# Moving four of ten block-pair loads from GpSimd's casting queue to ScalarE's queue and ScalarE's cast

## The chip, the cores and the metric

The kernel runs on one core of one Trainium2 chip. The metric is the device time of one execution in microseconds (us); of several runs the median is taken. The profile is of one execution on the same core, and its times count from the start of its span.

## The reference

A batch of 16 sequences of 512 rows and 768 columns is multiplied by one 768 x 768 weight, and each of the 12 heads (64 columns) is then rotated with a cosine and a sine that depend on the row alone. All inputs and the output are fp32.

```python
y = np.matmul(x, weight)                       # (16, 512, 768) x (768, 768)
y = y.reshape(batch, seq, n_heads, head_dim)
y1, y2 = y[..., :32], y[..., 32:]
out1 = y1 * cos1 - y2 * sin1
out2 = y2 * cos2 + y1 * sin2
out = np.concatenate([out1, out2], axis=-1).reshape(batch, seq, hidden)
```

## The kernel before

**Tiles and groups.** The 8192 rows are 64 tiles of 128 rows, numbered `i`. Four tiles make a group `g` (0 to 15; `LAST` is 15). A tile takes its 128 rows with a stride of 4, so all tiles of a group use the same rows of cosine and sine. A pair is half a group, written `(g, h)` with `h` 0 or 1.

**The way of an ordinary tile.** SP loads it in fp32 into one of ten `xs` buffers (`load`, L210). ScalarE casts it to fp16 (`cast`: CAST `xc<-xs`, L190). PE transposes it in 12 pieces into PSUM (`turn_rows`: `pt`, L271), ScalarE copies the result to SBUF (COPY `xt<-pt`, L190), and PE multiplies it with the weight (`one`, L362), two halves of the contraction on the two halves of the array's rows, in two lines that `both` interleaves.

**The way of a block pair.** The pairs in `BLOCKS`, (5,1) to (13,1) and (15,1), are not transposed by PE. A quarter of the pair at a time is loaded by a DMA whose order of rows and columns does the coarse part of the transpose (`load_quarter`, L225), each quarter on 32 partitions. DVE then transposes blocks of 32 x 32 (`turn_pair`: STREAM_TRANSPOSE `xp<-...`, L299), 32-bit words that each hold two fp16 numbers. Before that the pair must be fp16, and this is done in two ways:

- `"sp"` pairs (5, 7, 9, 11, 13 and 15) are loaded in fp32 by SP into one of three `xb` buffers, and ScalarE casts and reorders them into `xd` (`cast_pair`: CAST `xd<-xb`, L190).
- `"pool"` pairs (6, 8, 10 and 12) are loaded by GpSimd, and the DMA casts on its way into one of three fp16 buffers `xh`. DVE's transpose reads `xh` directly.

**After the product.** DVE multiplies PSUM with cosine and sine in one instruction (`rope`, L419, into `tq` or `w_raw`), GpSimd adds the two halves into one of four output buffers `ov` (L445, the groups listed as POOL). The additions of the last groups are cut smaller. Stores (`store`, L477) of half a group are issued from ScalarE's queue up to group 12, then from SP's. An output buffer is written again four groups later, once its store has landed.

**What sets the order.** The order of each engine's instructions is written out by a loop over the tiles; the helper `do` adds the waits that the named buffers call for. The end of a tile `i` of the main loop is:

```python
        bturns(i + (B_AHEAD if i < QB * (LAST - 2) else 9))
        ...
        turns(i + 1 + (T_AHEAD if i > QB else 2), 1)
        casts(i + 1 + (C_AHEAD if i > QB else 4), 1 + i % 2)
        pool_loads(i + P_AHEAD)
        for q in stores.get(i, ()):
            store(*q)
```

So at tile `i` ScalarE's stream holds the COPY of tile `i + 3`, the casts up to tile `i + 5` (a block pair's cast at its first tile) and then a store, if one is due there. `casts` also calls `pump`, which hands SP's loads out in a fixed order. GpSimd's quarters are issued 20 tiles ahead of the pair (`P_AHEAD`). A queue's instructions wait in order: what stands behind a waiting one waits too.

Of the kernel before, what the change touches and what calls it, by code (L numbers as in the profile page):

```python
# [10 lines left out]
FP32 = mybir.dt.float32  # L11
FP16 = mybir.dt.float16
# [4 lines left out]
class Flow:  # L17
# [24 lines left out]
    def do(self, e, make, reads=(), writes=(), dma=None, tick=True, after=0):  # L42
        need = {}
        for k in reads:
            for s, v in self.wrote.get(k, {}).items():
                need[s] = max(need.get(s, 0), v)
        for k in writes:
            for d in (self.wrote, self.readby):
                for s, v in d.get(k, {}).items():
                    need[s] = max(need.get(s, 0), v)  # L50
        if e == "pe":
            need.pop("pe", None)
            if after:
                need["pe"] = after
        waits = self.settle(e, need)
        for s, v in waits[:-1]:
            self.eng[e].wait_ge(self.sem(s), v)  # L57
        i = make(self.eng[e])
        if waits:
            s, v = waits[-1]  # L60
            i.wait_op(self.sem(s), v, "sem-ge")
        name, step = (dma, 16) if dma else (e, 1)
        self.sem(name)
        self.order[name] = len(self.order) + sum(self.count.values())
        at = self.count[name] + step
        if tick or dma:
            i.then_inc(self.sems[name], step)
            self.count[name] = at
            self.known[name, at] = dict(self.seen[e])
        for k in reads:  # L70
            d = self.readby.setdefault(k, {})
            d[name] = max(d.get(name, 0), at)
        for k in writes:
            self.wrote[k] = {name: at}
            self.readby[k] = {}
        return i
# [32 lines left out]
def kernel(  # L109
# [11 lines left out]
    f = Flow(nc, tc)  # L121
    do = f.do
    P = nc.NUM_PARTITIONS

    B, S, H = x.shape
# [4 lines left out]
    NQ = P // R  # L130
    NT = H // (2 * P)
    SB = S // P
    QB = 4
# [5 lines left out]

    BLOCKS = {}  # L140
    for g in range(5, 14):
        BLOCKS[g, 1] = "pool" if g % 2 == 0 and g >= 4 else "sp"
    BLOCKS[LAST, 1] = "sp"

    def sbuf(name, shape, dt):
        return nc.alloc_sbuf_tensor(name, shape, dt).ap()

    NX, NB, NBH, NC, NCP, NXT, NXP, NOV = 10, 3, 3, 5, 2, 8, 4, 4

    ident = sbuf("ident", [P, P], FP16)  # L150
    cold = sbuf("cold", [P, 512], FP16)
# [2 lines left out]
    w_raw = sbuf("w_raw", [P, NT, 2, H], FP32)  # L154
    w_sb = sbuf("w_sb", [P, NT, 2, H], FP16)
    xs_b = [sbuf(f"xs{i}", [P, H], FP32) for i in range(NX)]
    xb_b = [sbuf(f"xb{i}", [P, 2 * H], FP32) for i in range(NB)]
    xh_b = [sbuf(f"xh{i}", [P, 2 * H], FP16) for i in range(NBH)]
    xc_b = [sbuf(f"xc{i}", [P, H], FP16) for i in range(NC)]
    xd_b = [sbuf(f"xd{i}", [P, 2 * H], FP16) for i in range(NCP)]  # L160
    xt_b = [sbuf(f"xt{i}", [P, NT, 2, P], FP16) for i in range(NXT)]
# [21 lines left out]
    def ring(name, n, state={}):  # L183
        k = state.get((id(f), name), 0)
        state[id(f), name] = k + 1
        return k % n
# [6 lines left out]
    def where(i):  # L193
        g, s = divmod(i, QB)
        return QB * (g // SB) + s, g % SB

    def pair_of(i):
        return i // QB, (i % QB) // 2

    def is_block(i):  # L200
        return pair_of(i) in BLOCKS

    xs, xc, xT = {}, {}, {}
# [10 lines left out]
    def load_quarter(gh, q):  # L214
        g, h = gh
        b, r = where(g * QB + 2 * h)
        e = BLOCKS[gh]
        src = x[b : b + 2].rearrange("b (j a r) (q k) -> r q a (b j) k", r=SB, a=R, q=NQ)
        if q == 0:
            xs[gh] = ring("xh", NBH) if e == "pool" else ring("xb", NB)  # L220
        k = xs[gh]
        name = f"xh{k}" if e == "pool" else f"xb{k}"
        buf = xh_b[k] if e == "pool" else xb_b[k]
        dst = buf.rearrange("p (j k) -> p j k", j=2 * NQ)
        do(e, lambda eng: eng.dma_start(out=dst[ts(q, R)], in_=src[r, q]),  # L225
           writes=[f"{name}q{q}"], dma=name)
# [52 lines left out]
    def cast_pair(gh, e="act"):  # L279
        k = xs[gh]  # L280
        c = ring("xd", NCP)
        xc[gh] = c
        do(e, copy(e, xd_b[c].rearrange("p (t j e) -> p t j e", t=NT, e=2),
                   xb_b[k].rearrange("p (j t e) -> p t j e", t=NT, e=2)),
           reads=[f"xb{k}q{q}" for q in range(NQ)], writes=[f"xd{c}"])

    def turn_pair(gh):
        g, h = gh
        z = ring("xp", NXP)
        dst = xp_b[z].bitcast(FP32)  # L290
        if BLOCKS[gh] == "pool":
            k = xs[gh]
            src = xh_b[k].bitcast(FP32).rearrange("p (j t) -> p t j", t=NT)
            rd = [f"xh{k}q{q}" for q in range(NQ)]
        else:
            c = xc[gh]
            src, rd = xd_b[c].bitcast(FP32), [f"xd{c}"]
        v = xp_b[z].rearrange("p (t m e) -> p t e m", t=NT, e=2)
        do("dve", lambda eng: eng.transpose(out=dst, in_=src), reads=rd, writes=[f"xp{z}"])  # L299
        for s in (0, 1):  # L300
            xT[g * QB + 2 * h + s] = (
                lambda t, e, s=s: v[:, t, e, ts(s, P)], f"xp{z}")
# [211 lines left out]
    xs_used, xb_used = [0], [0]  # L514
# [38 lines left out]
    def castx(i, e):  # L553
        cast(i, e)
        xs_used[0] += 1
# [33 lines left out]
    pump()  # L589

    rows_on = [False]
    state = {"cast": 4, "turn": 4, "bturn": 0, "pool": 0}
    pairs = sorted(BLOCKS)
    pool_pairs = [p for p in pairs if BLOCKS[p] == "pool"]

    def casts(upto, most=NTILE):
        while state["cast"] < min(upto, NTILE) and most > 0:
            most -= 1
            i = state["cast"]
            state["cast"] += 1  # L600
            if not is_block(i):
                castx(i, "act")
            elif i % 2 == 0 and BLOCKS[pair_of(i)] == "sp" and pair_of(i) not in xc:
                cast_pair(pair_of(i))
                xb_used[0] += 1
            pump()

    def turns(upto, most=NTILE):
# [12 lines left out]
            turn_pair(gh)  # L621
            state["bturn"] += 1

    def pool_loads(upto):
        while state["pool"] < len(pool_pairs):
            gh = pool_pairs[state["pool"]]
            if gh[0] * QB + 2 * gh[1] >= upto:
                return
            for q in (0, 2, 1, 3):
                load_quarter(gh, q)  # L630
            state["pool"] += 1

    stores = {}
    for g in range(LAST):
        for h in (0, 2):
            i = QB * (g + 1) + h
            q = (g, h * H, (h + 2) * H, "act")
# [4 lines left out]
            elif g < LAST - 2:  # L642
                i = QB * (LAST - 2) + 2 * (g - LAST + 4) + h // 2
            else:
                q = q[:3] + ("sp",)
            stores.setdefault(i, []).append(q)

    C_AHEAD, T_AHEAD, B_AHEAD, P_AHEAD = 5, 3, 4, 20
    ROWS = QB * LAST - 2

    for i in (0, 1):
# [3 lines left out]
    mm0(2, CHUNKS[5])  # L655
    rope(0, U0[2])
    casts(6)
    for c in CHUNKS[:3]:
        mm0(3, c)
# [8 lines left out]
    for i in range(QB, NTILE):  # L668
        g, s = divmod(i, QB)
        us = units(g)  # L670
        done_to = (s + 1) * H
        rows_on[0] = QB <= i <= QB * LAST
        if i == QB * (LAST - 2) + 2:
            cast_pair((LAST, 1))
            xb_used[0] += 1
        if i < ROWS:
            if s % 2 == 0:
                for r in range(2):
                    lines[r].extend(walk(i // 2, r))
            for n in range(1, 4):  # L680
                both((i - QB) * 4608 + n * 1536)
                if n == (1 if i > QB else 2):
                    turns(i + T_AHEAD, 1)
        if i == ROWS:
            both(NTILE * 4608)
        for n, p in enumerate(pieces(g, s)) if i >= ROWS else ():
            a, z, _, bank = p
            if n == 1 and i < QB * LAST:
                turns(i + T_AHEAD, 1)
            for c in CHUNKS:  # L690
                mm_piece(i, p, c, c == CHUNKS[0], c == CHUNKS[-1],
                         tick=c == CHUNKS[-1])
            for u in us:
                if u[1] == z:
                    rope(g, u)
        bturns(i + (B_AHEAD if i < QB * (LAST - 2) else 9))
        if i == 2 * QB:
            do("pool", lambda eng: eng.tensor_copy(out=ident32, in_=ident),
               reads=["ident"], writes=["ident32", "wr20"])
        turns(i + 1 + (T_AHEAD if i > QB else 2), 1)  # L700
        casts(i + 1 + (C_AHEAD if i > QB else 4), 1 + i % 2)
        pool_loads(i + P_AHEAD)
        for q in stores.get(i, ()):
            store(*q)
        if g == LAST:
            if s == 2:
                store(g, 0, H, "sp")
            if s == 3:
                store(g, H, 2 * H, "act")
# [44 lines left out]
```

## Time and profile before

| | |
|---|---|
| Time, three runs | 149.74, 150.99, 157.2 us; median 150.99 |
| Span of the profiled execution | 148.2 us (its own time is not listed apart; the runs lie 1.5 us and more above the span) |
| Busy: PE, DVE, POOL, ACT | 140.8, 126.0, 121.8, 79.0 us |
| Granted clock of TensorE, mean | 0.998 |
| Moved by DMA | 51.67 MB, mean 349 GB/s |
| Queues, share of 16 DMA engines' span | SP 57.0%, ACT 35.9%, POOL 8.6% |
| Issue to landing, median: tiles, SP's quarters, POOL's quarters, ACT's stores | 16.4, 16.4, 12.1, 9.6 us |

L followed by a number is a line of the kernel. PE is TensorE's matmul, PEld its weight load, DVE VectorE, ACT ScalarE, POOL GpSimd, SP SyncE; a q behind a name (ACTq) is the engine's sequencer, where DMAs are issued. A line of the profile's groups gives line, engine, operation, output and input by name with the buffer number left out, shape and count; then the busy time and the mean of one in ns; then the engine's idle time just before, with what ended it. In a timeline a row is a start, a duration, the engine, the operation, a count where several follow each other, and in brackets the idle time before it. A DMA share over 1 means that packets overlap.

### The profile page before, as it was taken

The numbers are of one execution on the slowest core, as the hardware profiler recorded it, in microseconds if no ns is written. First come the engines' busy times: TensorE is split into PE (matmuls) and PEld (weight loads), VectorE is DVE, ScalarE is ACT, GpSimd is POOL, SyncE is SP. The second block draws the span as 40 slices with busy tenths as digits, with TensorE's granted clock in tenths as the row PEclk, the third lists the DMA queues.
The fourth block names the chain that finished last, engine by engine and source line by source line (L and its number), as shares of the span: only waits on it lengthen the run. The fifth ranks groups of instructions, "written<-read, shape, count | busy, mean of one in ns | idle before, by whom it ended". The sixth has DMA issues, their size and how long they took to land.

```text
span 148.2 us, 4422 instructions
## 1 busy us (share of the span) xinstructions
PE 140.8 (95%) x1948; PEld 112.7 (76%) x1948; DVE 126.0 (85%) x99; ACT 79.0 (53%) x94; POOL 121.8 (82%) x73
## 2 busy tenths in 40 slices
PE   6789999999999999999999999999999999999980
PEld 2335578888888888888888888888888888765860
DVE  0335998886988899899989998999989999999991
ACT  3453898777777933557261915375263919931010
POOL 1000396999999998999999999879699999999990
PEclk9999999999999999999999999999999999999999
DMA  3999999999999999999999999999999999998675
GB/s 124 352 395 403 402 406 398 373 379 296 317 366 330 352 353 277 294 408 287 319 355 397 379 323 358 365 408 324 381 365 337 411 409 416 410 408 333 264 297 180
DMA packets 27555, 51.67 MB, mean 349 GB/s; under 512 B 6160, under 2 KB 13072, under 8 KB 27536
## 3 DMA queue, kind: packets, MB, share of 16 engines
q1 hardware_dynamic: 15824, 28.84, 57.0%
q10 hardware_dynamic: 7360, 20.97, 35.9%
q0 software_dynamic: 4352, 1.57, 8.6%
q8 instruction: 15, 0.25, 0.7%
q14 instruction: 4, 0.03, 0.1%
HBM read 27.79 MB, written 25.17 MB: 357 GB/s over the span
## 4 chain that ended last, share of the span: by engine, by line
PE 78%; DVE 12%; DMA 4%; issue 1%; SPq 1%; DVEq 0%
PE py L362 68%; DVE tq L419 8%; PE py L337 5%; PE pt L271 4%; DMA w_raw<-in_weight_dram 4%; DVE w_raw L419 2%; SPq L210 1%; PE pt L256 1%; DVE ov L445 1%; DVE xs L419 1%; SPq L232 1%; DVE w_sb L190 0%; DVEq L57 0%; SPq L749 0%; SPq L119 0%
## 5 line engine op out<-in xcount | busy, mean ns | idle before, releaser
L445 POOL TENSOR_TENSOR ov<-tq 128x512 f32<-128x512 f32 (+3 forms) x35 | 76.8, 2220 | 20.1 <-DVE tq L419 20.1
L362 PE MATMUL py<-w_sb,xt 64*128 64x256 f16 (+1 forms) x864 | 81.5, 323 | 0.0
L419 DVE TENSOR_TENSOR tq<-py,csn 128x1024 f32<-128x1024 f32 (+2 forms) x51 | 74.4, 1496 | 4.6 <-PE py L362 4.5
L362 PEld LDWEIGHTS py<-w_sb,xt 64*128 64x128 f16 x864 | 59.9, 94 | 11.1 <-DVE tq L419 0.4
L190 ACT COPY xt<-pt 128x768 f16<-128x768 f16 x42 | 33.5, 801 | 47.5 <-PE pt L271 46.3
L362 PE MATMUL py<-w_sb,xp 64*128 64x512 f16 (+1 forms) x432 | 42.7, 323 | 0.0
L190 ACT CAST xc<-xs 128x768 f16<-128x768 f32 x44 | 38.8, 911 | 6.9 <-DMA xs<-in_x_dram 6.7
L419 DVE TENSOR_TENSOR w_raw<-py,csn 128x1024 f32<-128x1024 f32 (+1 forms) x22 | 35.3, 1606 | 4.4 <-PE py L362 4.0
L445 POOL TENSOR_TENSOR ov<-w_raw 128x1536 f32<-128x1536 f32 (+2 forms) x15 | 35.4, 2374 | 1.9 <-DVE w_raw L419 1.9
L362 PEld LDWEIGHTS py<-w_sb,xp 64*128 64x128 f16 x432 | 30.7, 94 | 5.0
L337 PE MATMUL py<-w_sb,xt 128*128 128x256 f16 (+1 forms) x102 | 17.0, 317 | 1.4 <-DVE w_sb L190 1.1
L271 PEld LDWEIGHTS pt<-ident,xc 64*128 64x128 f16 x456 | 14.9, 95 | 1.3 <-issue 0.2
L337 PEld LDWEIGHTS py<-w_sb,xt 128*128 128x128 f16 x102 | 9.2, 98 | 7.4 <-DVE w_sb L190 2.7
L271 PE MATMUL pt<-ident,xc 64*128 64x64 f16 x456 | 14.7, 190 | 0.0
L190 ACT CAST xd<-xb 128x1536 f16<-128x1536 f32 x6 | 9.8, 1634 | 0.0
L225 POOL DMA_DIRECT2D xh<-in_x_dram x16 | 9.4, 591 | 0.0
L190 DVE CAST w_sb<-w_raw 128x768 f16<-128x768 f32 x6 | 3.4, 559 | 3.6 <-DMA w_raw<-in_weight_dram 3.6
L299 DVE STREAM_TRANSPOSE xp<-xd 128x768 f32<-128x768 f32 x6 | 5.8, 970 | 0.0
L190 ACT COPY ov<-py 128x256 f32<-128x256 f32 x1 | 0.4, 372 | 10.1 <-POOL ov L445 10.1
L540 PE MATMUL py<-cold 128*128 128x512 f16 x12 | 4.3, 521 | 1.4 <-DVE cold L482 1.4
L190 DVE COPY xt<-pt 128x768 f16<-128x768 f16 x2 | 1.1, 558 | 4.8 <-PE pt L256 4.8
L299 DVE STREAM_TRANSPOSE xp<-xh 128x768 f32<-128x768 f32 x4 | 4.9, 1234 | 0.0
(23 smaller groups left out, 22.6 us busy)
## 6 DMA issues: line engine op xcount, KB each, us to landing
out_dram<-ov ACTq DMA_DIRECT2D x26, 768.0 KB, 9.6
xs<-in_x_dram SPq DMA_DIRECT2D x44, 384.0 KB, 16.4
xb<-in_x_dram SPq DMA_DIRECT2D x24, 192.0 KB, 16.4
out_dram<-ov SPq DMA_DIRECT2D x4, 768.0 KB, 6.2
w_raw<-in_weight_dram SPq DMA_DIRECT2D x6, 384.0 KB, 6.9
xh<-in_x_dram POOLq DMA_DIRECT2D x16, 96.0 KB, 12.1
out_dram<-ov SPq DMA_DIRECT2D x1, 384.0 KB, 2.3
out_dram<-ov ACTq DMA_DIRECT2D x1, 384.0 KB, 2.3
```

The source lines that it names most:

```text
L190: eng.copy(out=o, in_=i_) if e == "act" else eng.tensor_copy(out=o, in_=i_)
L210: do(e, lambda eng: eng.dma_start(out=xs_b[k], in_=x[b].rearrange("(p r) h -> r p h", r=SB)[r]), writes=[f"xs{k}"], dma=f"xs{k}")
L225: do(e, lambda eng: eng.dma_start(out=dst[ts(q, R)], in_=src[r, q]), writes=[f"{name}q{q}"], dma=name)
L232: do(e, lambda eng: eng.dma_start(out=w_raw[:, t, h], in_=wv[t, h]), writes=[f"wr{t}{h}"], dma=f"ov{t}_0" if h else f"xb{t}")
L256: do("pe", lambda eng: eng.transpose(pt[:, t, h, :], src[:, t, h, :], ident), reads=[f"xc{c}", "ident"], writes=[f"pt{k}"], tick=(t, h) == ...
L271: do("pe", lambda eng: eng.transpose(pts[r][:, t, h, :], src[rows, t, h, :], ident[rows, rows]), reads=[f"xc{c}", "ident"], writes=[f"pt{r ...
L299: do("dve", lambda eng: eng.transpose(out=dst, in_=src), reads=rd, writes=[f"xp{z}"])
L337: do("pe", lambda eng: eng.matmul(ps, get(t, h), w_sb[:, t, h, a - s * H : z - s * H], start=start, stop=stop), reads=[key, f"w{t}{h}"], w ...
L362: do("pe", lambda eng: eng.matmul(py[:, a:z], get(t, h)[rows], w_sb[rows, t, h, a - s * H : z - s * H], start=start, stop=not opens and en ...
L419: do("dve", lambda eng: eng.tensor_tensor(out=tq.rearrange("p j (h d) -> p j h d", d=D), in0=ps.rearrange("p (h d) -> p h d", d=D) .unsque ...
L445: do(adder, lambda eng: eng.tensor_tensor(out=ov_b[o][:, ds(c0, w)].rearrange("p (h t d) -> p h t d", t=2, d=HD), in0=tq[:, 0].rearrange(" ...
L540: do("pe", lambda eng: eng.matmul(py[:, ts(b, 512)], cold[:, 0:P], cold, start=True, stop=warmed[0] < WARM - 6), reads=["cold"], writes=[f ...
```

## The change

Pairs 6, 8, 10 and 12 are no longer loaded by GpSimd. They are loaded as fp32 quarters, as the `"sp"` pairs are, but from ScalarE's queue and into two `xb` buffers of their own (numbers 3 and 4). One quarter is issued at the end of each of four tiles, 14 to 11 tiles ahead of the pair's first tile, behind that tile's casts and ahead of its stores. ScalarE casts the pair into `xd` where the loop comes to its first tile, as for the `"sp"` pairs, and DVE transposes it from there. The buffers `xh` and the function `pool_loads` go.

```diff
-        BLOCKS[g, 1] = "pool" if g % 2 == 0 and g >= 4 else "sp"
+        BLOCKS[g, 1] = "act" if g % 2 == 0 else "sp"
...
-    NX, NB, NBH, NC, NCP, NXT, NXP, NOV = 10, 3, 3, 5, 2, 8, 4, 4
+    NX, NB, NBA, NC, NCP, NXT, NXP, NOV = 10, 3, 2, 5, 2, 8, 4, 4
...
-    xb_b = [sbuf(f"xb{i}", [P, 2 * H], FP32) for i in range(NB)]
-    xh_b = [sbuf(f"xh{i}", [P, 2 * H], FP16) for i in range(NBH)]
+    xb_b = [sbuf(f"xb{i}", [P, 2 * H], FP32) for i in range(NB + NBA)]
...
-            xs[gh] = ring("xh", NBH) if e == "pool" else ring("xb", NB)
+            xs[gh] = NB + ring("xa", NBA) if e == "act" else ring("xb", NB)
         k = xs[gh]
-        name = f"xh{k}" if e == "pool" else f"xb{k}"
-        buf = xh_b[k] if e == "pool" else xb_b[k]
+        name, buf = f"xb{k}", xb_b[k]
...
-        if BLOCKS[gh] == "pool":
-            k = xs[gh]
-            src = xh_b[k].bitcast(FP32).rearrange("p (j t) -> p t j", t=NT)
-            rd = [f"xh{k}q{q}" for q in range(NQ)]
-        else:
-            c = xc[gh]
-            src, rd = xd_b[c].bitcast(FP32), [f"xd{c}"]
+        c = xc[gh]
+        src, rd = xd_b[c].bitcast(FP32), [f"xd{c}"]
...
+    act_loads = {QB * g + 2 * h - 14 + n: ((g, h), q) for g, h in pairs if BLOCKS[g, h] == "act"
+                 for n, q in enumerate((0, 2, 1, 3))}
...
-            elif i % 2 == 0 and BLOCKS[pair_of(i)] == "sp" and pair_of(i) not in xc:
+            elif i % 2 == 0 and pair_of(i) not in xc:
                 cast_pair(pair_of(i))
-                xb_used[0] += 1
+                xb_used[0] += BLOCKS[pair_of(i)] == "sp"
...
-        pool_loads(i + P_AHEAD)
+        if i in act_loads:
+            load_quarter(*act_loads[i])
         for q in stores.get(i, ()):
             store(*q)
```

## The prediction

> **What bounds the kernel now.** I read the chain that ended last first, then the waits, the stretches, the ScalarE timeline and the DMA part of the page.
>
> ```profile
> PE 78%; DVE 12%; DMA 4%; issue 1%; SPq 1%; DVEq 0%
> ...
> L445 POOL TENSOR_TENSOR ov<-tq 128x512 f32<-128x512 f32 (+3 forms) x35 | 76.8, 2220 | 20.1 <-DVE tq L419 20.1
> ...
> L190 ACT CAST xd<-xb 128x1536 f16<-128x1536 f32 x6 | 9.8, 1634 | 0.0
> L225 POOL DMA_DIRECT2D xh<-in_x_dram x16 | 9.4, 591 | 0.0
> ...
> L299 DVE STREAM_TRANSPOSE xp<-xd 128x768 f32<-128x768 f32 x6 | 5.8, 970 | 0.0
> ...
> L299 DVE STREAM_TRANSPOSE xp<-xh 128x768 f32<-128x768 f32 x4 | 4.9, 1234 | 0.0
> ```
>
> PE is 78% of the chain. The chain in order of time shows PE without a break from 18.09 to 125.78 us, then DVE's products of the last groups until 144.9, then the last stores. So up to 125.78 us a saving on another engine is worth nothing, and every wait put on PE is paid in full. The stretches say who is near the limit beside PE:
>
> ```profile
> 50.00:67.00 17.00, 17.00 (x263) 14.68 (x261) 15.99 (x11) 8.52 (x11) 16.19 (x9) 1.00 1.12 339
> 67.00:83.00 16.00, 16.00 (x240) 13.72 (x237) 15.30 (x11) 7.56 (x10) 15.73 (x9) 1.00 1.12 345
> ...
> 116.00:126.00 10.00, 10.00 (x156) 8.48 (x154) 9.56 (x10) 6.47 (x8) 10.00 (x8) 1.00 1.03 412
> ```
>
> Columns: stretch, its length, busy us of PE, PEld, DVE, ACT and POOL, clock, DMA share, GB/s. PE is full; ACT is half idle; DVE and POOL are nearly full. The DMA share is over 1, that is, each of the 16 DMA engines always has a packet and some overlap: 1.12 while three queues (SP, ACT, POOL) carry data, 1.03 where two do. Bandwidth is as scarce as PE; it is hidden only because loads come early. The ScalarE timeline shows one group with a cast by DMA (89 to 94 us) and one with a ScalarE cast (97 to 102):
>
> ```profile
> 89.19 0.80 ACT L190 COPY xt<-pt 128x768 f16<-128x768 f16 x1 [3.52 <-PE pt L271]
> 91.31 0.80 ACT L190 COPY xt<-pt 128x768 f16<-128x768 f16 x1 [1.32 <-PE pt L271]
> 91.32 0.90 ACTq L477 DMA_DIRECT2D out_dram<-ov  x2
> ...
> 97.34 0.80 ACT L190 COPY xt<-pt 128x768 f16<-128x768 f16 x1 [3.62 <-PE pt L271]
> 98.04 1.64 ACT L190 CAST xd<-xb 128x1536 f16<-128x1536 f32 x1
> 99.47 0.38 ACTq L477 DMA_DIRECT2D out_dram<-ov  x1
> 99.55 0.82 ACT L190 COPY xt<-pt 128x768 f16<-128x768 f16 x1
> ```
>
> **What the change removes.** POOL loses 16 issues at 591 ns = 9.4 us, the last at 81 us. POOL's additions are not in the chain, and at 126.87 us it stood idle 0.32 us for DVE, so its backlog was gone before the tail: worth 0. DVE's four transposes go from 1234 to 970 ns, 1.06 us less; DVE waits for PE 8.5 us in all (4.5 and 4.0 in the waits): worth 0. If that cover were gone, both together could give at most the 1.06 us, since the additions can't end before DVE's products.
>
> **What it adds on ScalarE.** Four casts of 1634 ns = 6.5 us. Each falls between the two COPYs of its group, where ACT now idles 1.32 us; the second COPY slips by some 0.2 us, as at 99.55 (COPY period 8.15: 91.31 + 8.15 = 99.46). The tile of that COPY is first read by PE at 93.43 in the group at 89 (the timeline's matmuls), the COPY ends at 92.11: 1.3 us to spare, 1.1 after the slip. Cost 0, as in the groups that do it already. Sixteen issues on ACT's queue at 0.38 to 0.43 us (its store issues) = 6.4 us; they run beside ACT's arithmetic (the store issued at 91.32 overlaps the COPY), and at the dense tiles 12 to 15 ACT still idles 0.5 us of each 2.12. Cost 0. Queued behind them are a cast and the stores; nothing there has to wait for a buffer, since the third pair takes its buffer 10 us after the cast that frees it (67.3 against 57.3).
>
> **What it moves: the transfers.** HBM reads stay the same (768 KB a pair). A packet of a quarter takes 44.8 ns on average as fp32 of 768 bytes (SP's records) and 49.3 as a cast to 384 bytes: 4096 packets / 16 engines x 4.5 ns = 1.2 us of DMA time less. That is worth 0 by itself. But three queues become two, and the loads go behind and ahead of the stores in ACT's. The issue also comes later: POOL issued pair (8,1) at 46.1 to 47.9 us for a transpose at 77.3; now the four quarters are issued at tiles 20 to 23, the cast is due at tile 29.
>
> How queues share: between 49.0 and 50.5 us, with ACT and SP both backlogged, the packet records show 150 packets started from ACT's and 143 from SP's, so one each in turn. The Trainium skill, DMA: Bandwidth & Descriptors, Queues, rings and completion order, says the same: a DMA engine goes round the queues that have work, packet by packet, and keeps order within one. By that rule nothing of the sum below changes; were it by bytes, quarters would overtake.
>
> Now a ledger for ACT's queue. Two groups (16.3 us) give each DMA engine, from SP, 4 tiles x 8 packets of 3072 bytes and 4 quarters x 16 of 768; from ACT 4 stores x 16 of 3072 and, new, 4 quarters x 16. Means of the records are 129.5 and 44.8 ns, so SP's mean packet is (32 x 129.5 + 64 x 44.8) / 96 = 73 ns. A store then takes 16 x (129.5 + 73) = 3.24 us, a quarter 16 x (44.8 + 73) = 1.89. These include overlap with three queues; the two-queue share of 1.03 to 1.05 says to scale by 0.96: 3.11 and 1.81. First packet 4.0 us after the issue on an empty queue (store issued 22.95, first packets from 26.5; another 44.54, 49.0), landing 1.7 after the last. A store beside SP's loads would so take 4.0 + 3.1 + 1.7 = 8.8 us; the one at 22.95 took 9.1.
>
> In two groups ACT's queue needs 4 x 3.11 + 4 x 1.81 = 19.7 us of 16.3: **it falls 3.4 us behind every second group**, as long as SP has loads to give, and SP has (its issues are stretched to 5.9 us by a full queue, and its ten tile and three pair buffers let it run ahead).
>
> Run through from the store at 33.57, in the order of the code (issue times: stores as in the timeline, quarters at ACT's place for the tile):
>
> ```
> pair     4th quarter issued  queue done with it  landed  cast due  late
> (6,1)    44.2                52.2                53.9    57.3      -
> (8,1)    59.2                69.1                70.8    73.6      -
> (10,1)   75.9                88.8                90.5    89.9      0.6
> (12,1)   92.2                108.5               110.2   106.2     4.0
> ```
>
> The cast waits in order, so the second COPY of the group waits behind it, then PE; 1.1 us is free. Pair (12,1) costs 4.0 - 1.1 = 2.9 us. The page's instruction fetches (queue 8, 0.7%) over the 70 us of the ledger add 0.5: **3.4 us**. What is late next: everything after it, at its old distance; the tail's chain starts from PE's last group, so nothing swallows it.
>
> Bounds of this unseen wait: unscaled means (3.24, 1.89) give 2.2 late at (10,1) and 5.3 at (12,1), 1.1 + 4.2 = 5.3 us. Scaled by the full 1.12 (2.87, 1.67) the last quarter lands less than 1.1 us late: 0. I take 3.4, because two queues are what the new kernel has.
>
> The sum: span 148.2 + 3.4 = 151.6. The times shown (149.74, 150.99, 157.2) lie at least 1.5 us above that span; against their median, 150.99 + 3.4 = **154.4**.
>
> **Rivals.**
> (a) Nothing happens. Quarters land in time; PE stays unbroken; 150.99, or 149.9 with DVE's 1.06. For it: the gap is 1.1 us of tolerance against an estimate, and the DMA work is a little less; it decides as long as a store takes less than 2.9 us of the queue. Against: the ledger's two-queue rate. The Trainium skill, same page, Issuing engines are not separate DMA queues, says that DMAs of all issuing engines share the same 16 engines and only issue time is saved: by it 150.99. The DMA share of 1.12 bears out the sharing; it leaves out the order within a queue.
> (b) ACT's queue gets less than its turn. A store at 3.6 us (what 9.6 us of median landing leaves with 4.0 and 1.7 taken off is 3.9, with three queues) makes (10,1) 5.1 late and (12,1), after that shift of 4.0, 6.7: 4.0 + 5.6 = 9.6 us, 160.6. Against: the even turns at 49 us. Output buffers would not wait even then: the last store ahead, of group 7, lands at 120.5, and POOL's write over it (112.26 now) has moved to 121.9.
> (c) POOL's 9.4 us reach the end: POOL has no gap from 108.84 to 126.87, so it paces DVE there if DVE waits for a product buffer. Worth 3 us only if that backlog set the start of the tail: 147.9. Against: no wait of DVE for POOL is listed, and the 0.32 us gap.
> (d) ScalarE itself is late: were the issues not hidden, a group would have 1.63 + 4 x 0.4 = 3.2 us more between its COPYs, against 1.32 of idle time and 1.1 to spare: 0.8 x 4 = 3.2 us, 154.2. Against: the store issues overlap, and ACT waits 46.3 us for PE's transposes.
>
> **How the numbers follow.** Forecast 0.46, (a) 0.36, (b) 0.07, (c) 0.07, (d) 0.04. Two per cent is 3.0 us, about what a measurement of this kernel can tell from no change. Slower: nearly all of the forecast, (b) and (d) 0.54; within: (a) and the forecast's lower edge 0.39; faster: (c) 0.07. The forecast's own range is 153 to 157; with (a), 0 from the lower bound and DVE's 1.06, and some of (b), 149.8 to 158.5.
>
> **What would show it.** Right: a row of ACT waiting for DMA before the xd cast, longest at the last new pair (about 106 us); PE waiting some us for the COPY of xt behind it; PE's chain broken near 93 and 109 and not before 75; ACT's store landing up from 9.6 us to 11 or more, SP's loads down from 16.4; POOL busy 112 us, four more casts of 1.63, all ten transposes at 0.97. Wrong: PE unbroken until 125.8 and no wait of the cast (then a), a wait of POOL for stores (b), DVE in the tail starting sooner (c), COPYs late without a DMA wait (d).

## The result and the profile after

The changed kernel took 157.35 us (median of 4 runs, 155.15 to 158.65), the kernel before 153.5 beside it (149.74 to 157.2); some runs of either ran in a slower state, among them the profiled run of the changed kernel (158.65 us) and that of the fp32 quarters on GpSimd's queue below (156.36 us), so these two traces show more lost time than the ratios, which leave such runs out. The ratio is 1.039, 95% interval 1.028 to 1.050: slower, by more than the forecast's 2.3%. Beside the experiments below the kernel before had medians of 150.2 to 150.65 over 7 to 25 runs. The profiled execution of the changed kernel has a span of 156.9 us, 8.7 more than before; 3.9% of the time before would be some 6 us, so of what follows the places and the causes carry over to the other runs, but not each size.

The waits of the changed kernel (who waited for whom: total us, times, longest us), cut to the new ones:

```profile
ACT xd L189 <- DMA xb<-in_x_dram: 10.6, 4, 3.8
...
PE py L355 <- ACT xt L189: 5.7, 3, 2.4
...
POOL ov L438 <- DMA out_dram<-ov: 1.2, 2, 0.9
```

ScalarE's four new casts wait for their quarters, 10.6 us in all; PE waits behind them three times. The ScalarE timeline shows how one of these goes, at the last new pair:

```profile
109.89 0.80 ACT L189 COPY xt<-pt 128x768 f16<-128x768 f16 x1 [3.49 <-PE pt L269]
114.47 1.57 ACT L189 CAST xd<-xb 128x1536 f16<-128x1536 f32 x1 [3.78 <-DMA xb<-in_x_dram]
114.48 2.05 ACTq L470 DMA_DIRECT2D out_dram<-ov  x2
115.94 0.80 ACT L189 COPY xt<-pt 128x768 f16<-128x768 f16 x1
```

and the PE timeline its end (duration, count, and in brackets the idle time):

```profile
114.09 0.38 PE L355 MATMUL py<-w_sb,xt 64*128 64x512 f16 x1
116.89 5.16 PE L355 MATMUL py<-w_sb,xt 64*128 64x512 f16 x40 [2.42 <-ACT xt L189]
```

The cast stands 3.78 us for its data, the second COPY of the group behind it, and PE behind the COPY. The stretch right after has a lower clock (stretch, length, busy us of PE, PEld, DVE, ACT and POOL, clock, DMA share, GB/s):

```profile
117.00:121.00 4.00, 4.00 (x30) 2.43 (x29) 2.23 (x2) 1.32 (x2) 2.97 (x2) 0.59 1.00 404
```

Set matmul by matmul beside the trace of before, PE is 0.49 us late from the start (the first weights landed later; in two later runs this part is 0.11 and 0.72 us, so it is not the change's), then the lag grows at four places only: by 1.62 us at pair (8,1)'s cast, 2.29 at (10,1)'s, 2.69 at (12,1)'s, and 1.65 in the stretch at 0.59 of the clock. The sum is 8.74; the span grew by 8.7. The lines of the page that answer to those shown before:

```profile
DMA 45%; PE 33%; DVE 11%; ACTq 4%; issue 2%; SPq 1%; ACT 1%; DVEq 0%
...
L189 ACT CAST xd<-xb 128x1536 f16<-128x1536 f32 x10 | 16.2, 1620 | 10.6 <-DMA xb<-in_x_dram 10.6
...
L292 DVE STREAM_TRANSPOSE xp<-xd 128x768 f32<-128x768 f32 x10 | 9.7, 972 | 3.5 <-ACT xd L189 3.5
```

```profile
out_dram<-ov ACTq DMA_DIRECT2D x26, 768.0 KB, 14.3
xs<-in_x_dram SPq DMA_DIRECT2D x44, 384.0 KB, 15.7
xb<-in_x_dram SPq DMA_DIRECT2D x24, 192.0 KB, 15.6
xb<-in_x_dram ACTq DMA_DIRECT2D x16, 192.0 KB, 13.5
```

The chain now runs through the quarters' loads (40% of it `xb<-in_x_dram`) more than through PE (33%). ScalarE's stores land in 14.3 us instead of 9.6.

Why are the quarters late? Two rows of the same kernel gave the lead: the DMA engines are busy all the time and yet move half as much.

```profile
35.00:38.00 3.00, 3.00 (x55) 2.68 (x53) 2.50 (x2) 2.31 (x3) 3.00 (x1) 1.00 1.06 198
49.00:55.00 6.00, 6.00 (x87) 5.26 (x84) 5.27 (x5) 4.60 (x5) 5.08 (x2) 1.00 1.11 235
```

In these stretches most packet records are quarters' packets of 768 bytes: 259 of 388 in the first, all of SP's quarters, and 996 of 1201 in the second, 594 of them ScalarE's. For the whole middle the measure used from here on is the rate between 33 and 110 us, from the last column of one such row for each kernel:

```profile
33.00:110.00 77.00, 77.00 (x1179) 66.31 (x1177) 70.66 (x46) 42.58 (x51) 72.35 (x33) 1.00 1.11 347
```

```profile
33.00:110.00 77.00, 73.72 (x1122) 64.85 (x1119) 67.13 (x43) 44.97 (x51) 60.62 (x20) 1.00 1.06 344
```

The first is before, the second after. They look alike, but in the kernel before the view counts a packet of the casting queue by the 384 bytes it writes, not the 768 it reads. Its 4096 data packets in those 77 us stand for 20 GB/s more read, so before moved 367 GB/s of what has to be read and written in memory, after 344.

### The profile page after: what moved, and what is told of

Same layout as the page of the kernel before. It is cut to its first block, busy times and chain, and to the rows that moved or that the text cites. A ratio compares the mean times of both kernels' runs of the same rounds, so it can differ in the third digit from the quotient of the medians.

```text
span 156.9 us, 4426 instructions
## 1 busy us (share of the span) xinstructions
PE 143.2 (91%) x1948; PEld 115.9 (74%) x1948; DVE 125.9 (80%) x99; ACT 85.4 (54%) x98; POOL 113.0 (72%) x57
## 4 chain that ended last, share of the span: by engine, by line
DMA 45%; PE 33%; DVE 11%; ACTq 4%; issue 2%; SPq 1%; ACT 1%; DVEq 0%
DMA xb<-in_x_dram 40%; PE py L355 25%; DVE tq L412 8%; DMA w_raw<-in_weight_dram 4%; PE py L330 4%; ACTq L470 3%; PE pt L269 2%; DVE w_raw L412 2%; ACTq L223 1%; ACT xd L189 1%; SPq L209 1%; PE pt L254 1%; DVE ov L438 1%; DVE xs L412 1%; SPq L230 1%
## 5 line engine op out<-in xcount | busy, mean ns | idle before, releaser
L355 PE MATMUL py<-w_sb,xt 64*128 64x512 f16 (+1 forms) x864 | 84.3, 327 | 5.7 <-ACT xt L189 5.7
L355 PEld LDWEIGHTS py<-w_sb,xt 64*128 64x128 f16 x864 | 61.6, 95 | 17.8 <-issue 7.9
L355 PEld LDWEIGHTS py<-w_sb,xp 64*128 64x128 f16 x432 | 32.6, 94 | 3.3
L189 ACT CAST xd<-xb 128x1536 f16<-128x1536 f32 x10 | 16.2, 1620 | 10.6 <-DMA xb<-in_x_dram 10.6
L269 PE MATMUL pt<-ident,xc 64*128 64x64 f16 x456 | 16.0, 190 | 0.0
L292 DVE STREAM_TRANSPOSE xp<-xd 128x768 f32<-128x768 f32 x10 | 9.7, 972 | 3.5 <-ACT xd L189 3.5
L254 PEld LDWEIGHTS pt<-ident,xc 128*128 128x128 f16 x36 | 2.1, 98 | 2.7 <-ACT xc L189 1.9
L533 PEld LDWEIGHTS py<-cold 128*128 128x128 f16 x12 | 1.4, 127 | 3.4 <-issue 1.8
## 6 DMA issues: line engine op xcount, KB each, us to landing
out_dram<-ov ACTq DMA_DIRECT2D x26, 768.0 KB, 14.3
```

The lines of the kernel that those rows point to most:

```text
L189: eng.copy(out=o, in_=i_) if e == "act" else eng.tensor_copy(out=o, in_=i_)
L254: do("pe", lambda eng: eng.transpose(pt[:, t, h, :], src[:, t, h, :], ident), reads=[f"xc{c}", "ident"], writes=[f"pt{k}"], tick=(t, h) == ...
L269: do("pe", lambda eng: eng.transpose(pts[r][:, t, h, :], src[rows, t, h, :], ident[rows, rows]), reads=[f"xc{c}", "ident"], writes=[f"pt{r ...
L355: do("pe", lambda eng: eng.matmul(py[:, a:z], get(t, h)[rows], w_sb[rows, t, h, a - s * H : z - s * H], start=start, stop=not opens and en ...
L533: do("pe", lambda eng: eng.matmul(py[:, ts(b, 512)], cold[:, 0:P], cold, start=True, stop=warmed[0] < WARM - 6), reads=["cold"], writes=[f ...
```

## The experiments

Nine further kernels ran. Theory A: only the lead of the issue is too short. B: ScalarE's queue falls behind for good. C: the cast or the width costs by itself. In the later runs C is split: P, the transfers that write only 32 partitions are slow; V, the doubled bytes are, wherever they go; T, the taking of turns between queues, as in the prediction's ledger. The last five versions, from "All 128 partitions" on, leave out the order of a pair's rows and columns (the very last also half of its data), so their output for those pairs is not the reference's; they measure the transfers alone.

**Earlier issue.**

```diff
-    act_loads = {QB * g + 2 * h - 14 + n: ...
+    act_loads = {QB * g + 2 * h - 18 + n: ...
```

> The quarters are issued 18 to 15 tiles ahead of the pair instead of 14 to 11. Theory A (the casts wait because a quarter needs 14 to 17 us from issue to landing on ScalarE's queue, and the lead was some 14 us): the lead grows by 4 tiles, about 8.2 us; the waits of the four xd casts, 10.6 us after the change, go to 0, PE runs unbroken to about 126 us, TensorE's clock shows no dip, span 148 to 149.5, time as before the change. Rival B (ScalarE's queue falls further behind at every pair, whatever the lead): the first pairs are free, the last still wait 2 us or more, span 151 to 154. Rival C (the loss is the ScalarE cast itself or the width of the loads): no change against the changed kernel, span 155 or more.

Measured: no wait of an xd cast is left, as A said, but 154.0 us against 150.2, ratio 1.026 (1.020 to 1.031), span 152.3. The rate is 343 GB/s, as after the change:

```profile
33.00:110.00 77.00, 76.23 (x1162) 65.91 (x1160) 69.23 (x44) 47.34 (x53) 61.33 (x20) 1.00 1.06 343
```

Half of the loss has moved to the end. PE is 2.0 us late: 0.7 from the start, 0.5 at 41 us, which stays unexplained, and 0.7 at 92 us, behind a store's issue on ScalarE that took 2.54 us at 89.46. The other 2.1 us come after PE, where the last additions and stores run beside stores that are still queued: store to landing is 14.6 us, and the last ones take 3 to 4 us where before they took 2. A is half the story, B as stated is wrong (no pair waits), C not excluded.

**Later issue**, the same line with 12.

> The quarters are issued 12 to 9 tiles ahead, two tiles (4.1 us) later than in the change. Theory A: each cast waits up to 4.1 us longer than the 0.84, 2.59, 3.38 and 3.78 us of the change, so some 20 to 26 us in all, PE stands 1.1 us less per pair, and the span grows by 8 to 16 us to about 165 to 172. Rival B: as theory A for the last pairs, less for the first. Rival C: span unchanged at 155 to 157.

Measured: 165.73 us in one run, span 163.9. The direction is A's, the size less: casts wait 16.0 us, not 20 to 26, probably since PE, held back, asks for less and the DMA catches up. PE lags at all four pairs, and twice the clock falls.

**The cast alone, queue unchanged.** The quarters go as fp32 through GpSimd's queue, 20 tiles ahead as before; ScalarE casts them.

```diff
-        BLOCKS[g, 1] = "act" if g % 2 == 0 else "sp"
+        BLOCKS[g, 1] = "pool" if g % 2 == 0 else "sp"
```

> The four pairs are loaded as fp32 and cast by ScalarE as in the change, but the quarters stay on GpSimd's queue, 20 tiles ahead as before the change (two buffers). It does the cast part of the change alone. Theory A and B: no wait of a cast, span 148 to 149.5, time as before. Rival C (cast or fp32 width costs by themselves): span 151 or more, with ScalarE's COPYs late or the DMA slower, though no cast waits.

Measured: 155.3 us, ratio 1.031 (1.022 to 1.040), rate 349 GB/s. A and B fail: the quarters are early (7.9 us to landing), one pair cast alone waits, 0.5 us, and time is lost all the same. The wait has gone to SP's loads:

```profile
ACT xc L189 <- DMA xs<-in_x_dram: 37.2, 16, 4.4
```

Before, the casts of ordinary tiles waited 6.7 us, all at the start. One thing more than the cast changed: the trace has these quarters in packets of 3072 and 4608 bytes, not 768. So this run alone does not tell how much of SP's loss lies in the turns.

**All pairs on SP's queue**, five buffers; ScalarE's queue holds stores alone.

```diff
-        BLOCKS[g, 1] = "act" if g % 2 == 0 else "sp"
+        BLOCKS[g, 1] = "sp"
-    NX, NB, NBA, ... = 10, 3, 2, ...
+    NX, NB, NBA, ... = 10, 5, 0, ...
```

> All ten pairs go through SP's queue, with five buffers, and ScalarE casts them; ScalarE's queue holds only stores again. Theory A: the queue matters, not the bytes: no cast waits for its quarters as long as SP runs ahead far enough, stores land in some 9 us again, span 148 to 150. Rival B': total DMA bandwidth with two queues is short, so SP falls behind and casts of tiles or pairs wait: span 151 to 156.

Measured: 160.94 us, ratio 1.071 (1.063 to 1.079), rate 341 GB/s. Stores land in 9.0 us, but tile casts wait 21.6 us and pair casts 7.3. So whichever queue carries the fp32 quarters, the core's DMA moves 341 to 349 GB/s; the queue chooses who pays, and how much.

**All 128 partitions for the same bytes.**

```diff
+        if e == "act":
+            src = x[b : b + 2].rearrange("b (p r) (q c) -> r q p b c", r=SB, q=NQ)
+            dst = buf[:, ts(q, 2 * H // NQ)].rearrange("p (b c) -> p b c", b=2)
...
```

> The changed kernel, but each quarter of ScalarE's queue goes to all 128 partitions (two runs of 768 bytes each) instead of eight runs to each of 32: same bytes, same 256 packets of 768 bytes, same times of issue; the pair's rows and columns are not put in order, so the values of these four pairs are not the reference's. Theory P (a transfer that writes only 32 partitions reaches half of the ports of the SBUF, at some 200 to 235 GB/s, and four fp32 pairs double the bytes that go that way against the cast): the DMA rate between 33 and 110 us, counted in packets read, comes back from 342 to 365 GB/s or near it, the quarters land 3 us or more sooner, the four waits of the xd casts (10.6 us) fall to 2 us or less, span 148 to 151. Rival V (the doubled bytes themselves, wherever they go): nothing changes, waits 9 to 12 us, span 154 to 157. Rival T (turns of the queue and its order, as in the prediction's ledger): nothing changes either, since packets and order are the same.

Measured: 151.69 us, ratio 1.007 (1.003 to 1.011); the profiled run took 150.39 us, span 148.6. The row of the middle:

```profile
33.00:110.00 77.00, 77.00 (x1176) 65.17 (x1171) 69.97 (x46) 47.11 (x53) 64.42 (x21) 1.00 1.06 369
```

369 GB/s with the same bytes, packet size, queue and order, and waits of the xd casts of 1.6 us instead of 10.6: V fails, T as the whole cause too, P holds. One cast is still late; the short lead is what is left.

**The same with a lead of 18.**

> As the run before it (values of the four pairs out of order, all 128 partitions), with the quarters issued 18 to 15 tiles ahead. Theory P: the lead takes the waits away and the width the slower DMA, so the last stores are no longer late: PE unbroken, span 148 to 149.5, time as before the change. Rival V: as with the lead of 18 alone, span 151.5 to 153, with the end set by stores that the DMA delivers late. Rival T: 151 to 153 as well.

Measured: 150.42 us, ratio 1.000 (0.996 to 1.003), span 148.5, 371 GB/s, no cast late. With both causes gone the change costs nothing, and gains nothing.

**All ten pairs wide.**

> The changed kernel with all 40 quarters, SP's too, written to all 128 partitions (values of the ten pairs out of order). Theory P: no narrow transfer is left; the DMA rate between 33 and 110 us exceeds 365 GB/s and no stretch of some us falls to 200 to 235; no cast waits; span 147.5 to 149. Rival V: rate 340 to 350, waits as in the change, span 154 to 157.

Measured: 150.19 us, ratio 0.998 (0.996 to 1.001), 394 GB/s, no cast late though the lead is 14. This run also tells a packet's size from where it lands: of the single microseconds of the middle, those in which 50 to 70% of the bytes are in packets of 768 bytes moved 376 GB/s here (8 of them) and 245 in the changed kernel (7). Between 110 and 126 us the DMA engines are busy 0.63 to 0.89 of the time, where the kernel before stays over 1. Still no faster: PE is unbroken and sets the time.

**Four turns instead of sixteen.** A quarter as 64 packets of 3072 bytes, to partitions 0 to 63 or 64 to 127.

```diff
+        if e == "act":
+            rows, col = ts(q % 2, 64), q // 2
+            src = x[b + col].rearrange("(p r) h -> r p h", r=SB)[r][rows]
+            dst = buf[rows, ts(col, H)]
...
```

> The changed kernel with each quarter of ScalarE's queue as 64 packets of 3072 bytes to 64 partitions (values of the four pairs out of order). Theory P: 64 partitions that lie together reach no more ports than 32, but a quarter is four packets for each DMA engine in place of sixteen; rate and waits stay near those of the change if the port is the limit: waits 6 to 11 us, span 152 to 157. Rival T: a quarter takes 4 turns instead of 16, so ScalarE's queue runs through its quarters in 0.8 us each instead of 2.2 to 2.9; the casts do not wait, span 148 to 150.

Measured: 154.46 us, span 152.7, 352 GB/s:

```profile
33.00:110.00 77.00, 77.00 (x1181) 66.62 (x1178) 69.96 (x45) 48.36 (x54) 64.39 (x21) 1.00 1.05 352
```

It is one run, and three of the 25 runs of the kernel before took 154.15 to 154.4 us, so its time proves little; its trace says more. Each theory got half: the quarters do land sooner (8.5 us) and xd casts wait only 1.4 us, as the turns of T say, but the rate stays low, as P says, and ordinary tiles wait:

```profile
ACT xc L189 <- DMA xs<-in_x_dram: 24.1, 13, 4.8
```

**The same 64 packets, other 64 partitions**: 32 to 95.

```diff
-            rows, col = ts(q % 2, 64), q // 2
+            rows, col = ds(32, 64), q // 2
-            dst = buf[rows, ts(col, H)]
+            dst = (xz if q % 2 else buf)[rows, ts(col, H)]
```

> As the run with 64 packets of 3072 bytes a quarter (values of the four pairs out of order), but every quarter goes to partitions 32 to 95 instead of 0 to 63 or 64 to 127; the odd quarters go to a scratch tile, and the rows of the pair's buffers that get no data are cleared at the start. Packets, bytes and the number of partitions are the same. Theory P (ports, which by the Trainium skill, SBUF - State Buffer, Door 1, go by bits of the partition's number, so that 0 to 63 lie on half of them and 32 to 95 on all): the DMA rate between 33 and 110 us rises from 350 to 365 GB/s or more, the tile casts no longer wait from about 18 us on (24 us of waits in the run with 0 to 63), span 148 to 150. Rival N (the number of partitions or rows of a transfer counts): rate 345 to 355, waits of the tile casts 18 to 26 us, span 151.5 to 154.

Measured: 150.32 us, ratio 0.999 (0.996 to 1.002), span 148.5:

```profile
33.00:110.00 77.00, 77.00 (x1181) 66.36 (x1178) 69.95 (x45) 48.62 (x55) 64.44 (x21) 1.00 1.05 371
```

```profile
ACT xc L190 <- DMA xs<-in_x_dram: 7.1, 4, 2.4
```

Rival N falls. Not how many partitions, but which: 0 to 63 and 64 to 127 by turns give 352 GB/s, 32 to 95 give 371, with the same packets, bytes and number of partitions. The difference shows inside the single run with 0 to 63 too. Of its middle, take the microseconds in which SP's narrow packets hold under 20% of the bytes: where ScalarE's quarters (told from its stores by the order of issue) hold over 35% of the bytes it moved 317 GB/s (13 of them), where they hold under 5%, 391 (42). In the run with 32 to 95 these are 364 (13) and 387 (45). Two things differ beside the partitions: the rows read are 32 to 95 as well, each read twice, and half of the quarters land in a scratch tile. No run takes these apart from the partitions.

## Why the prediction was right and wrong

**Right.** The path: a late quarter holds the cast, the cast the second COPY, the COPY PE, with 1.1 us to spare. At (8,1) the cast came 2.69 us after its place behind the first COPY and PE lost 1.62; at (12,1) 3.88 and 2.69. That tolerance was good to 0.1 us. The places near 93 and 109 us were named too (PE, by then late, stopped at 95.9 and 114.5); the stop at 78.0 was not. The zeros hold, taken together: with the same four casts and sixteen issues on ScalarE and GpSimd relieved, the two wide versions without a late cast take 1.000 and 0.998 of the time before. So the cast on ScalarE is free, rival (d) falls, and GpSimd's 9.4 us and DVE's 1.06 are worth nothing, rival (c). Rival (a) falls with the result. Rival (b) left its sign, GpSimd waiting 1.2 us for stores, but PE's lag has no step there, and the turns were even: between 49 and 55 us 607 data packets started from ScalarE's queue and 594 from SP's. (In the prediction's stretch of 49.0 to 50.5 us of the kernel before, the records hold 135 and 139 data packets, not 150 and 143, and its lower bound is 2.89 and 1.69 us, not 2.87 and 1.67; neither changes its sum.)

**Wrong, first step: "What it moves: the transfers", the 1.2 us of DMA time less.** It compared the packets' own durations, 44.8 against 49.3 ns, took the sum for the DMA's capacity, and put the doubling of the written bytes at nothing. What counted is where the bytes land. A quarter writes 32 partitions; while many such packets are written the core moves 198 to 235 GB/s with all DMA engines "busy", against 402 between 8 and 20 us of the same trace. The cast by DMA had halved those bytes for four pairs. The rate fell from 367 to 344 GB/s: over 77 us 1.8 MB, or some 5 us of transfers, that come late. The Trainium skill has the rule: SBUF — State Buffer, Door 1, says that a DMA's bandwidth goes by how many of 16 ports its partitions reach and that 0 to 63 reach only the 8 that 0 to 31 do. The last two runs agree, 352 against 371 GB/s. The prediction weighed the page on queues and not this one, which spoke against the change.

**Wrong, second step: the ledger's term for a quarter.** It priced a turn by the mean packets of the kernel before, 73 ns for SP's and 44.8 for a quarter's. Between 49 and 55 us of the changed kernel SP's data packets took 107 ns in the mean and ScalarE's, nearly all of quarters, 66. Set at 1.81 us, the quarters of (6,1) followed each other by 2.2 to 2.9 us, and the first packets of the store ahead, issued at 34.11, came 5.6 us after its issue, not 4.0. So the fourth quarter of (6,1) landed at 58.75 instead of 53.9, of (8,1) at 76.83 instead of 70.8, and of (10,1) at 95.46 instead of 90.5. Three pairs cost PE time, 6.6 us, where the sum had one and 2.9. The ledger's upper end, 5.3, was nearer, yet it had left out the cause. So the direction was in good part luck: the wide version keeps the ledger's turns, packets, order and lead, without the narrow writes, and is 0.7% slower, 1 us, where the sum had 3.4.

**Wrong, third: the clock.** The sum had no term for it. After the third stop of PE the granted clock was half for 3.4 us, which cost 1.65 us.

**Half right: the queue.** Rivals and forecast spoke of the order within ScalarE's queue. The four versions with narrow fp32 quarters that ran several times show that any queue loses (1.026 to 1.071); the order decides whether pairs, tiles or the last stores are late.

## What to carry to other kernels

When a kernel's DMA engines are always busy, cost a moved transfer by the bytes it writes and the partitions it writes them to, not by the duration of its packets: here sixteen quarters of 192 KB cost nothing on partitions 32 to 95 and some 4 us, in one run, on 0 to 63 and 64 to 127. A busy share near 1 with a low GB/s is the sign to look for, stretch by stretch. And before moving a load to another queue, ask what stays if the order were perfect: here an earlier issue took all the waits of the casts away and still left the kernel 2.6% slower.

## What the runs showed that was not expected

Narrow transfers slow the other queues as well: in the middle the whole core lost 23 GB/s, although three quarters of its bytes were wide, and tile loads of SP waited when GpSimd's fp32 quarters were narrow (37.2 us) or ScalarE's lay on 0 to 63 and 64 to 127 (24.1).

An issue can hold its engine. In the changed kernel ScalarE's issues took 0.3 to 0.6 us as a rule. Twelve took 1.1 to 2.8 us, eleven of them with six or seven of its transfers outstanding and one with four; a queue that is full would do this, but no view shows the queue's depth. At 89 us of the run with the longer lead such an issue held back a COPY.

TensorE's granted clock fell to half for 3.4 us after PE had stood 2.42 us, but not after stops of 1.26 and 2.02 us. The eleven traces fit one rule. The clock changes only at whole steps of 3.413 us, counted from the moment when it first became full. Each of the 17 falls (11 of them behind PE's last matmul) follows a step at full clock in which PE stood 1.99 us or more, and no step in which it stood 1.77 us or less is followed by one. The border of a step cut the stop of 2.02 us into 0.5 and 1.5; of the stop of 2.42 us, 2.37 lay in one step.
